# Decay rates of a gated recurrence in a PSUM bank, and the gates' plus-one on ScalarE

## The chip, the cores and the metric

The kernel runs on one core of one Trainium2 chip. The metric is the device time in microseconds (us) of one execution, as the median over runs.

Names used below: PE is TensorE, whose weight loads are listed apart as PEld; DVE is VectorE, ACT is ScalarE, POOL is GpSimd, and SP is SyncE, which issues most of the DMAs. SBUF is the working memory. PSUM is the memory that PE writes its products to, and here it is handled in eight banks of 128 partitions by 512 float32 numbers.

## The reference

One block of a decoder on a sequence of 512 positions with 1024 channels, all in float32. Cut to what matters here:

```python
h = rmsnorm(x, norm1_g[l])
z = h @ w_in[l] + b_in[l]
z_glu, z_rx, z_rg, z_ga, z_gb = jnp.split(z, split_idx, axis=-1)
u = z_glu[..., :D_CONV] * jax.nn.sigmoid(z_glu[..., D_CONV:])
u = causal_depthwise_conv(u, conv_dw_w[l], conv_dw_b[l])
u = jax.nn.silu(layernorm(u, conv_ln_g[l], conv_ln_b[l]))
y_a = u @ conv_w_out[l] + conv_b_out[l]
xb = causal_depthwise_conv(z_rx, lru_conv_w[l], lru_conv_b[l])
hb = rg_lru(xb, ...)
y_b = (hb * jax.nn.gelu(z_rg, approximate=True)) @ lru_w_out[l]
m = jax.nn.sigmoid(z_ga) * y_a + jax.nn.sigmoid(z_gb) * y_b
x = x + m @ w_mix_out[l]
```

The first conv has 31 taps, the second 4. A second norm, a SwiGLU feed-forward of 2816 channels and a last norm follow. The recurrence `rg_lru` works on 1280 channels. It forms two gates r and i from block-diagonal products of xb, and from the parameter `lru_lambda` the decay of each channel:

```python
log_a = -LRU_C * r * jax.nn.softplus(-lam)
a = jnp.exp(log_a)
mult = jnp.sqrt(-jnp.expm1(2.0 * log_a))
```

With these h[t] = a[t] * h[t-1] + mult[t] * i[t] * xb[t], and LRU_C is 8. So `softplus(-lam)`, one number for each channel, is needed once for the whole kernel (1280 numbers, held as 128 partitions by 10). The change concerns these ten columns, and one operation of the ten gate units.

## The kernel before

**Layout.** Channels lie on the 128 partitions and the 512 positions along the free dimension. Every matrix is cut into tiles of 128 output channels. To keep float32 accuracy, each operand is split into a high part and a low remainder, and each product is three matmuls (high by high, high by low, low by high; `mm3`, L539). The high part is a cast on ACT (`split_to`, L133), the remainder a subtraction on DVE or POOL (L129). For most weight chunks of w_in POOL does the subtraction.

**Order of the work.** After a hand-ordered start (L638 to L669: the input norm, its transposes, the first four tiles u0 and u1 of the input product), a written list `ORDER` says in which order the units come: `u` (two input tiles and the gated product, `glu`, L796), `rx` (an input tile and the four-tap conv, `rx`, L810), `g` (the gates of one of ten tiles, `gates`, L845), `r` (the recurrence of one tile, `recur`, L879), `rg`, `gb` and `ga` (further input tiles with their activations, L895 and L888). It begins `u0 u1 rx0 rx1 gb0 rx2 u2 g0 rx3 gb1 g1` and ends `rg9 ga2 ga3 ga4 ga5 ga6 ga7`. Then come the products with lru_w_out (`yb`), conv_w_out (`co`, `ya`), the mixing product (`mx`), and the feed-forward (`f`, `fr`, `o`).

**The side work.** The 31-tap conv, 240 instructions `scalar_tensor_tensor` on DVE (L733) for four pairs of tiles, and after it the layer norm are a generator, `beside()` (L721). Each unit of `ORDER` advances it by some steps (`run_beside(n)`, L789), and from rg5 on its steps are ordered behind the product of an earlier `rg` unit (`behind`, L787 and L899). Its two column sums are matmuls by ones (`column_mean`, L740, tiles `lnmp` and `lnvp`), each called a fixed count of steps (`LAG` = 12) after its input.

**Who orders the queues.** The text gives a priority; the framework fixes the order in each engine's queue when the kernel is built, from its own estimate of times. Each engine then works through its queue in order and waits at its head for semaphores. Outside the hand-ordered parts, work that stands later in the text can so come earlier in a queue.

**PSUM.** A pool `psum` of six banks (`bank`, tag mm) serves the input tiles, the gates and the recurrence, and a pool of two (`bank2`) serves the conv accumulators. A bank is held from its first writer to its last reader.

**What the change touches.** L674 to L699 compute the rates ahead of the first unit: x = -lambda, its absolute value, e = exp(-|x|) on ACT (L680), s = e / (2 + e), a polynomial in s squared of nine terms (L686 to L690) that makes log(1 + e), softplus = max(x, 0) + 2 * s * polynomial (L691), then `c8` and `c4`, the rates scaled by -4 and -2 (L694, L695). L699 halves the two gate biases into `bh`. All are instructions on 128x10 numbers in the SBUF tile `sm`, DVE except L680. The first readers are the gates of tile 0: L865 and L866 (Tanh, with `bh`), L869 (Exp, with `c8`) and L870 (Tanh, with `c4`).

In `gates` four DVE instructions follow: L871 makes r_ = (A + 1) * r_ in the PSUM bank, L872 the gated input, L873 writes A = r_ + 1 to SBUF, and L874 th = (A + 1) * r_, which `recur` turns into the factor `mult` (L882). L874 is the last reader of that bank. The copies of parts of xb that the gates of other tiles need (`ext_in`, L828) go by DMA through SP (L840); the gates read them in their fourth and later matmuls (L860).

Of the kernel before, what the change touches and what calls it, by code (L numbers as in the profile page):

```python
# [22 lines left out]
LRU_C = 8.0  # L23
# [4 lines left out]
NR = DR // P  # L28
# [68 lines left out]
def tile_block(ctx, tc, a, out):  # L97
    nc = tc.nc
    pool = lambda name, bufs, **k: ctx.enter_context(tc.tile_pool(name=name, bufs=bufs, **k))
    consts = pool("consts", 1)  # L100
# [16 lines left out]
    def bank(name):  # L117
        return psum.tile([P, T], F32, tag="mm", name=name)
# [4 lines left out]
    vec, act, pe, pool_e = nc.vector, nc.scalar, nc.tensor, nc.gpsimd  # L123
# [547 lines left out]

    lam = par[:, col["lru_lambda"] : col["lru_lambda"] + NR]  # L674
    sm = consts.tile([P, 6, NR], F32, name="sm")
    ab, e, s, s2, po, c4 = (sm[:, i, :] for i in range(6))
    vec.tensor_scalar(out=e, in0=lam, scalar1=-1.0, scalar2=None, op0=ALU.mult)
    vec.tensor_tensor(out=ab, in0=lam, in1=e, op=ALU.max)
    vec.tensor_scalar(out=c4, in0=e, scalar1=0.0, scalar2=None, op0=ALU.max)
    act.activation(e, ab, AF.Exp, scale=-1.0)  # L680
    vec.tensor_scalar(out=s, in0=e, scalar1=2.0, scalar2=None, op0=ALU.add)
    vec.reciprocal(s, s)
    vec.tensor_tensor(out=s, in0=s, in1=e, op=ALU.mult)
    vec.tensor_tensor(out=s2, in0=s, in1=s, op=ALU.mult)
    n_terms = 9
    vec.tensor_scalar(out=po, in0=s2, scalar1=1.0 / (2 * n_terms - 1), scalar2=1.0 / (2 * n_terms - 3), op0=ALU.mult, op1=ALU.add)  # L686
    for k in range(n_terms - 3, -1, -1):
        vec.tensor_tensor(out=po, in0=po, in1=s2, op=ALU.mult)
        vec.tensor_scalar(out=po, in0=po, scalar1=1.0 / (2 * k + 1), scalar2=None, op0=ALU.add)
    vec.tensor_tensor(out=po, in0=po, in1=s, op=ALU.mult)  # L690
    vec.scalar_tensor_tensor(out=c4, in0=po, scalar=2.0, in1=c4, op0=ALU.mult, op1=ALU.add)  # L691

    c8 = consts.tile([P, NR], F32, name="c8")
    vec.tensor_scalar(out=c8, in0=c4, scalar1=-LRU_C / 2, scalar2=None, op0=ALU.mult)  # L694
    vec.tensor_scalar(out=c4, in0=c4, scalar1=-LRU_C / 4, scalar2=None, op0=ALU.mult)  # L695

    bh = consts.tile([P, 2, NR], F32, name="bh")
    for g, name in enumerate(("lru_ba", "lru_bx")):
        vec.tensor_scalar(out=bh[:, g, :], in0=par[:, col[name] : col[name] + NR], scalar1=0.5, scalar2=None, op0=ALU.mult)  # L699

    def b_in(m):
        return pc("b_in", m)
# [86 lines left out]
    def run_beside(n):  # L789
        with tc.issue_after(behind[0]) if behind[0] else nullcontext():  # L790
            for _ in range(n):
                next(side, None)
        behind[0] = behind[1] or behind[0]


    def glu(j):  # L796
        pv = in_mm(GLU + j)
        run_beside(6 if j > 1 else 0)
        pg = in_mm(GLU + 8 + j)
        sg = shortt(f"sg{j}")  # L800
        act.activation(sg, pg, AF.Sigmoid, bias=b_in(GLU + 8 + j))
        uj = longt(f"u{j}")
        vec.scalar_tensor_tensor(out=uj, in0=pv, scalar=b_in(GLU + j), in1=sg, op0=ALU.add, op1=ALU.mult)
        u.append(uj)
        run_beside(6 if j else 0)
# [4 lines left out]
    def rx(j):  # L810
        ps = in_mm(RX + j)
        act.activation(ps, ps, AF.Identity, bias=b_in(RX + j))
        o = longt(f"xb{j}")
        lw = lambda s: pc("lru_conv_w", (KL - 1 - s) * NR + j)
        act.activation(o, ps, AF.Identity, scale=lw(0), bias=pc("lru_conv_b", j))
        for s in range(1, KL):
            vec.scalar_tensor_tensor(out=o[:, s:], in0=ps[:, : T - s], scalar=lw(s), in1=o[:, s:], op0=ALU.mult, op1=ALU.add)
# [27 lines left out]
    def gates(j):  # L845
        hv, lv = (gate_view(v[:, 0, :]) for v in weights(f"gate{j}"))
        j5 = j % 5
        banks = []
        for g in range(2):
            ps = bank(f"g{j}_{g}")  # L850
            (wh, oh), (wl, ol) = ((v[:, g, 0, :], v[:, g, 1, :]) for v in (hv, lv))
            xh, xl = xbp[j]
            mms = [(wh, xh), (wh, xl), (wl, xh)]
            if j5 % 2:
                eh, el = ext[j]
                mms += [(l[:MANY], r[:MANY]) for l, r in ((oh, eh), (oh, el), (ol, eh))]
            else:
                mms.append((oh[: 3 * FEW], ext[j][0][: 3 * FEW]))
            for k, (l, r) in enumerate(mms):
                pe.matmul(ps, l, r, start=k == 0, stop=k == len(mms) - 1)  # L860
# [8 lines left out]
        act.activation(A, th, AF.Exp, scale=c8[:, j : j + 1], bias=c8[:, j : j + 1])  # L869
        act.activation(r_, th, AF.Tanh, scale=c4[:, j : j + 1], bias=c4[:, j : j + 1])  # L870
        vec.scalar_tensor_tensor(out=r_, in0=A, scalar=1.0, in1=r_, op0=ALU.add, op1=ALU.mult)  # L871
        vec.scalar_tensor_tensor(out=xb[j], in0=i_, scalar=1.0, in1=xb[j], op0=ALU.add, op1=ALU.mult)  # L872
        vec.tensor_scalar(out=A, in0=r_, scalar1=1.0, scalar2=None, op0=ALU.add)  # L873
# [21 lines left out]
    def rg(j):  # L895
        ps = in_mm(RG + j)
        act.activation(ps, ps, AF.Gelu_apprx_tanh, bias=b_in(RG + j))
        product = vec.tensor_tensor(out=ps, in0=hs[j], in1=ps, op=ALU.mult)
        behind[1] = product.ins if j >= BEHIND else None  # L899
        y.append(split(f"y{j}", ps, vec))  # L900
# [4 lines left out]
    for kind, j in ORDER:  # L905
        next(f_sums_steps, None)
        if kind == "u":
            glu(j)
        elif kind == "rx":
            rx(j)  # L910
            run_beside(4)
        elif kind == "g":
            gates(j)
        elif kind == "r":
            recur(j)
        elif kind == "rg":
            rg(j)
            run_beside(6)
        elif kind == "gb":
            sig(GB, j, sgb, "sgb")  # L920
            run_beside(6)
        else:
            sig(GA, j, sga, "sga")
            run_beside(8)


    for j in range(8):
        ws = w_tiles(f"lo{j}_0", 5) + w_tiles(f"lo{j}_1", 5)
        ps = bank(f"yb{j}")
# [121 lines left out]
    for n, j in enumerate(mixq.order()):  # L1051
        ws = w_tiles(f"co{j}", ND)
        ps = bank(f"ya{j}")
# [410 lines left out]
```

## Time and profile before

| what | value |
|---|---|
| median of 3 runs | 799.04 us (797.56 to 799.54) |
| the profiled execution: span from first to last instruction | 797.3 us |
| that execution's own time beside its span | not given apart from the span; the median lies 1.7 us above it |
| mean granted clock of PE | 0.997 of full speed |
| busy share of the span: PE, DVE, ACT, POOL | 99%, 87%, 59%, 45% |
| instructions | 12582 |

How to read the rows that follow. A row of the timeline is: start in us, duration in us (of the whole group where it ends in x2 or more), engine, line of the kernel, operation, tile written <- tiles read, shapes, count; in square brackets the idle time of that engine just before it, and what ended it. A row of grouped instructions ends with busy us and mean ns of one, then idle time before. A row of waits is: engine, what waited, what it waited for, us in total, times, longest. A row of the table by stage is: the stretch in us, its length, then for PE, PEld, DVE, ACT and POOL the busy us with the count of instructions, and the granted clock, the DMA share and GB/s. PE's weight loads run beside its matmuls.

### The profile page before, as it was taken

Reading aid. Unit: us, or ns where it says so; the run is one execution under the profiler, and the core shown is the slowest. Engines: PE = TensorE matmul, PEld = TensorE weight load, DVE = VectorE, ACT = ScalarE, POOL = GpSimd, SP = SyncE. Lnnn points to the kernel's source line nnn. Section 1 sums busy time; section 2 is a strip of 40 time slices with the busy share of each in tenths; the row PEclk is TensorE's granted clock in tenths of the full one; section 3 lists DMA queues with packets and bytes.
Section 4 is the critical chain, followed back from the end, with each engine's and each line's share of the span. In section 5 each row is a group of like instructions: output and inputs, shape, how many; then the busy total and the mean of one; then the engine's idle time right before and its main releaser. Section 6 shows DMA issues by size and latency. Waiting matters only on the chain.

```text
span 797.3 us, 12582 instructions
## 1 busy us (share of the span) xinstructions
PE 786.5 (99%) x4374; PEld 689.1 (86%) x4374; DVE 696.8 (87%) x1097; ACT 473.2 (59%) x674; POOL 359.9 (45%) x347
## 2 busy tenths in 40 slices
PE   8999999999999999999999999999999999999996
PEld 7988888888888888888887898999999999888885
DVE  5899999999998997985799968898877798999956
ACT  7546688777679654562326467554555555556743
POOL 2576778788779988853360482113312221000000
PEclk9999999999999999999999999999999999999998
DMA  7745566577776786879887887588988898778652
GB/s 216 196 127 175 162 190 195 179 238 229 200 247 202 243 272 212 281 232 296 266 309 238 277 263 230 150 273 264 355 298 289 301 326 294 239 236 258 206 171 105
DMA packets 181074, 188.13 MB, mean 236 GB/s; under 512 B 14119, under 2 KB 142035, under 8 KB 181011
## 3 DMA queue, kind: packets, MB, share of 16 engines
q1 hardware_dynamic: 172195, 156.66, 63.1%
q0 software_dynamic: 8672, 30.41, 11.0%
q8 instruction: 34, 0.56, 0.3%
q10 hardware_dynamic: 144, 0.26, 0.1%
q14 instruction: 29, 0.24, 0.1%
HBM read 145.48 MB, written 38.80 MB: 231 GB/s over the span
## 4 chain that ended last, share of the span: by engine, by line
PE 83%; DVE 9%; DMA 4%; issue 2%; ACT 2%; SPq 0%; DVEq 0%; ACTq 0%
PE z L539 35%; PE fr L1218 24%; PE or L991 13%; PE f L539 3%; PE g L860 3%; PE mxr L991 3%; DMA raw_lo<-in_lru_w_out_dram 1%; DMA raw_co<-in_conv_w_out_dram 1%; DMA mxws<-in_w_mix_out_dram 1%; PE fr L1262 1%; DVE hl_co L129 1%; PE yb L539 1%; DVE hl_mxb L129 1%; DVE mxws L129 1%; DVE sga L1056 1%
## 5 line engine op out<-in xcount | busy, mean ns | idle before, releaser
L733 DVE SCALAR_TENSOR_TENSOR cv<-u,par,cv 128x511 f32<-128x511 f32 (+17 forms) x240 | 162.6, 728 | 1.1 <-ACT cv L730 0.9
L129 POOL TENSOR_TENSOR hl_in<-raw_in,hl_in 128x1024 fp32r<-128x1024 f32 x51 | 123.2, 2422 | 63.6 <-ACT hl_in L133 45.1
L129 POOL TENSOR_TENSOR fws<-fws 128x256 f32<-128x256 f32 x120 | 104.6, 874 | 78.6 <-DMA fws<-in_ffn_w_dram 72.9
L398 POOL DMA_DIRECT2D ot<-fwso x21 | 15.3, 731 | 164.4 <-DVE fwso L129 156.7
L1218 PE MATMUL fr<-hs_0h,hl_ft 128*128 128x256 f32 x320 | 59.2, 283 | 0.0
L133 ACT CAST hl_in<-raw_in 128x1024 fp32r<-128x1024 f32 x51 | 53.2, 1043 | 3.2 <-POOL fws L394 1.3
L129 DVE TENSOR_TENSOR hl_ft<-raw_ft,hl_ft 128x1024 fp32r<-128x1024 f32 x39 | 47.5, 1218 | 5.5 <-ACT hl_ft L133 5.5
L1218 PEld LDWEIGHTS fr<-hs_0h,hl_ft 128*128 128x128 f32 x320 | 50.6, 192 | 0.0
L133 ACT CAST hl_ft<-raw_ft 128x1024 fp32r<-128x1024 f32 x40 | 41.8, 1046 | 13.2 <-PE fr L1218 9.9
L129 DVE TENSOR_TENSOR hl_fb<-raw_fb,hl_fb 128x1024 fp32r<-128x1024 f32 x30 | 36.7, 1222 | 14.6 <-ACT hl_fb L133 13.8
L1218 PE MATMUL fr<-hs_0l,hl_ft 128*128 128x256 f32 x160 | 45.3, 283 | 0.0
L133 ACT CAST hl_fb<-raw_fb 128x1024 fp32r<-128x1024 f32 x30 | 31.5, 1050 | 20.8 <-PE fr L1218 13.3
L539 PE MATMUL z<-h10h,hl_in 128*128 128x512 f32 (+1 forms) x110 | 41.4, 378 | 0.0
L539 PE MATMUL z<-h17h,hl_in 128*128 128x512 f32 (+1 forms) x110 | 41.1, 376 | 0.0
L539 PE MATMUL z<-h11h,hl_in 128*128 128x512 f32 (+1 forms) x110 | 41.1, 376 | 0.0
L539 PE MATMUL z<-h13h,hl_in 128*128 128x512 f32 (+1 forms) x110 | 41.1, 376 | 0.0
L539 PE MATMUL z<-h14h,hl_in 128*128 128x512 f32 (+1 forms) x110 | 41.1, 376 | 0.0
L539 PE MATMUL z<-h15h,hl_in 128*128 128x512 f32 (+1 forms) x110 | 41.1, 376 | 0.0
L539 PE MATMUL z<-h16h,hl_in 128*128 128x512 f32 (+1 forms) x110 | 41.1, 376 | 0.0
L539 PE MATMUL z<-h12h,hl_in 128*128 128x512 f32 (+1 forms) x110 | 41.1, 375 | 0.0
L133 ACT CAST hl_ob<-raw_ob 128x1024 fp32r<-128x1024 f32 (+1 forms) x23 | 23.4, 1016 | 23.4 <-PE or L991 10.5
L394 POOL TENSOR_TENSOR fws<-fws 128x256 f32<-128x256 f32 x40 | 31.6, 792 | 2.8
(962 smaller groups left out, 2640.6 us busy)
## 6 DMA issues: line engine op xcount, KB each, us to landing
raw_in<-in_w_in_dram SPq DMA_DIRECT2D x52, 512.0 KB
fws<-in_ffn_w_dram SPq DMA_DIRECT2D x80, 256.0 KB
raw_ft<-fs SPq DMA_DIRECT2D x34, 512.0 KB
fs<-fws SPq DMA_DIRECT2D x23, 512.0 KB
ot<-fwso POOLq DMA_DIRECT2D x21, 512.0 KB, 6.0
fwso<-in_ffn_w_dram POOLq DMA_DIRECT2D x40, 256.0 KB, 7.1
fs<-fws POOLq DMA_DIRECT2D x17, 512.0 KB, 4.9
raw_ob<-in_ffn_w_dram SPq DMA_DIRECT2D x33, 256.0 KB
```

The costliest lines, as they stand in the source:

```text
L129: return eng.tensor_tensor(out=o, in0=x, in1=y, op=ALU.subtract)
L133: copy(h, full)
L394: eng.tensor_tensor(out=q11, in0=q22, in1=q11, op=ALU.add)
L398: return queue.dma_start(dest, raw.rearrange("p (m n) -> p m n", m=dest.shape[1]))
L539: pe.matmul(ps, l, r, start=i == 0, stop=i == n - 1)
L733: vec.scalar_tensor_tensor(out=acc[c][:, s:], in0=u[c][:, : T - s], scalar=dw(c, s), in1=acc[c][:, s:], op0=ALU.mult, op1=ALU.add)
L860: pe.matmul(ps, l, r, start=k == 0, stop=k == len(mms) - 1)
L991: pe.matmul(banks[i], l_[:, ts], r_, start=start and n == 0, stop=stop and n == 2, skip_group_check=again)
L1056: vec.scalar_tensor_tensor(out=o, in0=ps, scalar=pc("conv_b_out", j), in1=o, op0=ALU.add, op1=ALU.mult)
L1218: pe.matmul(ps[:, HALVES[i]], lw[:, c, :], rx_, start=not (again or i or c or m), stop=bool(i and c == 3 and m == 2), skip_group_check=True,)
L1262: pe.matmul(self.r4[:, HALVES[i]], lw, rx_, start=not (i or c or m), stop=bool(i and c == 3 and m == 2), skip_group_check=True)
```

## The change

The rates move into a function `decay_rates`, called in the loop over `ORDER` after unit rx0 and its four steps of side work. Four of its intermediate columns lie in a bank of the six (`bank("sm")`), the others in SBUF, so that each DVE instruction has an operand in PSUM. The polynomial is now one `scalar_tensor_tensor` for each term, (po + coefficient) * s2, in place of a multiplication and an addition. ACT takes over 2 + e, the square, the first coefficient and the two halvings. In `gates` the plus-one of L873 becomes a Copy with a bias on ACT.

```diff
-    lam = par[:, col["lru_lambda"] : col["lru_lambda"] + NR]
-    sm = consts.tile([P, 6, NR], F32, name="sm")
-    ab, e, s, s2, po, c4 = (sm[:, i, :] for i in range(6))
...
-    act.activation(e, ab, AF.Exp, scale=-1.0)
-    vec.tensor_scalar(out=s, in0=e, scalar1=2.0, scalar2=None, op0=ALU.add)
-    vec.reciprocal(s, s)
...
-    vec.tensor_scalar(out=po, in0=s2, scalar1=1.0 / (2 * n_terms - 1), scalar2=1.0 / (2 * n_terms - 3), op0=ALU.mult, op1=ALU.add)
-    for k in range(n_terms - 3, -1, -1):
-        vec.tensor_tensor(out=po, in0=po, in1=s2, op=ALU.mult)
-        vec.tensor_scalar(out=po, in0=po, scalar1=1.0 / (2 * k + 1), scalar2=None, op0=ALU.add)
-    vec.tensor_tensor(out=po, in0=po, in1=s, op=ALU.mult)
-    vec.scalar_tensor_tensor(out=c4, in0=po, scalar=2.0, in1=c4, op0=ALU.mult, op1=ALU.add)
...
+    sm = consts.tile([P, 4, NR], F32, name="sm")
+    c4, c8 = (consts.tile([P, NR], F32, name=n) for n in ("c4", "c8"))
     bh = consts.tile([P, 2, NR], F32, name="bh")
-    for g, name in enumerate(("lru_ba", "lru_bx")):
-        vec.tensor_scalar(out=bh[:, g, :], in0=par[:, col[name] : col[name] + NR], scalar1=0.5, scalar2=None, op0=ALU.mult)
+
+    def decay_rates():
+
+        lam = par[:, col["lru_lambda"] : col["lru_lambda"] + NR]
+        ps = bank("sm")
+        neg, ab, inv, po = (ps[:, i * NR : i * NR + NR] for i in range(4))
+        lo, e, s, s2 = (sm[:, i, :] for i in range(4))
+        vec.tensor_scalar(out=neg, in0=lam, scalar1=-1.0, scalar2=None, op0=ALU.mult)
+        vec.tensor_tensor(out=ab, in0=lam, in1=neg, op=ALU.max)
+        vec.tensor_scalar(out=lo, in0=neg, scalar1=0.0, scalar2=None, op0=ALU.max)
+        act.activation(e, ab, AF.Exp, scale=-1.0)
+        act.activation(inv, e, AF.Copy, bias=2.0)
+        vec.reciprocal(inv, inv)
+        vec.tensor_tensor(out=s, in0=inv, in1=e, op=ALU.mult)
+        act.activation(s2, s, AF.Square)
+        n_terms = 9
+        act.activation(po, s2, AF.Copy, scale=1.0 / (2 * n_terms - 1))
+        for k in range(n_terms - 2, 0, -1):
+            vec.scalar_tensor_tensor(out=po, in0=po, scalar=1.0 / (2 * k + 1), in1=s2, op0=ALU.add, op1=ALU.mult)
+        vec.scalar_tensor_tensor(out=po, in0=po, scalar=1.0, in1=s, op0=ALU.add, op1=ALU.mult)
+        vec.scalar_tensor_tensor(out=po, in0=po, scalar=2.0, in1=lo, op0=ALU.mult, op1=ALU.add)
+        vec.tensor_scalar(out=c8, in0=po, scalar1=-LRU_C / 2, scalar2=None, op0=ALU.mult)
+        vec.tensor_scalar(out=c4, in0=po, scalar1=-LRU_C / 4, scalar2=None, op0=ALU.mult)
+        for g, name in enumerate(("lru_ba", "lru_bx")):
+            act.activation(bh[:, g, :], par[:, col[name] : col[name] + NR], AF.Copy, scale=0.5)
...
-        vec.tensor_scalar(out=A, in0=r_, scalar1=1.0, scalar2=None, op0=ALU.add)
+        act.activation(A, r_, AF.Copy, bias=1.0)
         vec.scalar_tensor_tensor(out=th, in0=A, scalar=1.0, in1=r_, op0=ALU.add, op1=ALU.mult)
...
             rx(j)
             run_beside(4)
+            if j == 0:
+                decay_rates()
```

More of the change, by code (lines that the diff above doesn't have):

```diff
@@ L670, in tile_block @@
     h1 = parts_of(h1p)
-    lam = par[:, col["lru_lambda"] : col["lru_lambda"] + NR]
-    sm = consts.tile([P, 6, NR], F32, name="sm")
-    ab, e, s, s2, po, c4 = (sm[:, i, :] for i in range(6))
-    vec.tensor_scalar(out=e, in0=lam, scalar1=-1.0, scalar2=None, op0=ALU.mult)
-    vec.tensor_tensor(out=ab, in0=lam, in1=e, op=ALU.max)
-    vec.tensor_scalar(out=c4, in0=e, scalar1=0.0, scalar2=None, op0=ALU.max)
-    act.activation(e, ab, AF.Exp, scale=-1.0)
-    vec.tensor_scalar(out=s, in0=e, scalar1=2.0, scalar2=None, op0=ALU.add)
@@ L682, in tile_block @@
-    vec.reciprocal(s, s)
-    vec.tensor_tensor(out=s, in0=s, in1=e, op=ALU.mult)
-    vec.tensor_tensor(out=s2, in0=s, in1=s, op=ALU.mult)
-    n_terms = 9
-    vec.tensor_scalar(out=po, in0=s2, scalar1=1.0 / (2 * n_terms - 1), scalar2=1.0 / (2 * n_terms - 3), op0=ALU.mult, op1=ALU.add)
-    for k in range(n_terms - 3, -1, -1):
-        vec.tensor_tensor(out=po, in0=po, in1=s2, op=ALU.mult)
-        vec.tensor_scalar(out=po, in0=po, scalar1=1.0 / (2 * k + 1), scalar2=None, op0=ALU.add)
-    vec.tensor_tensor(out=po, in0=po, in1=s, op=ALU.mult)
@@ L691, in tile_block @@
-    vec.scalar_tensor_tensor(out=c4, in0=po, scalar=2.0, in1=c4, op0=ALU.mult, op1=ALU.add)
-    c8 = consts.tile([P, NR], F32, name="c8")
-    vec.tensor_scalar(out=c8, in0=c4, scalar1=-LRU_C / 2, scalar2=None, op0=ALU.mult)
-    vec.tensor_scalar(out=c4, in0=c4, scalar1=-LRU_C / 4, scalar2=None, op0=ALU.mult)
-    bh = consts.tile([P, 2, NR], F32, name="bh")
-    for g, name in enumerate(("lru_ba", "lru_bx")):
-        vec.tensor_scalar(out=bh[:, g, :], in0=par[:, col[name] : col[name] + NR], scalar1=0.5, scalar2=None, op0=ALU.mult)
+    sm = consts.tile([P, 4, NR], F32, name="sm")
```

## The prediction

> **What bounds the kernel now.** I read the page first, then the busy time by stage, then what TensorE (PE) waited for.
>
> ```profile
> span 797.3 us, 12582 instructions
> PE 786.5 (99%) x4374; PEld 689.1 (86%) x4374; DVE 696.8 (87%) x1097; ACT 473.2 (59%) x674; POOL 359.9 (45%) x347
> ```
>
> ```profile
> core 0: us, PE busy (x) PEld busy (x) DVE busy (x) ACT busy (x) POOL busy (x), PEclk, DMA share, GB/s
> 0.00:25.00 25.00, 22.31 (x160) 20.77 (x161) 13.56 (x38) 18.32 (x43) 7.85 (x9) 1.00 0.74 215
> ```
>
> ```profile
> 686.00:787.00 101.00, 101.00 (x447) 83.66 (x446) 90.22 (x145) 60.39 (x91) 0.72 (x1) 1.00 0.65 208
> 787.00:797.30 10.30, 3.65 (x17) 2.68 (x15) 5.12 (x11) 3.26 (x9) 0.00 (x0) 0.80 0.27 102
> ```
>
> ```profile
> 25.00:37.70 12.70, 12.70 (x102) 12.43 (x101) 11.64 (x30) 5.11 (x6) 7.70 (x4) 1.00 0.82 220
> 37.70:68.90 31.20, 31.20 (x139) 25.84 (x138) 29.64 (x47) 14.34 (x20) 20.11 (x14) 1.00 0.46 132
> 68.90:231.00 162.10, 162.10 (x715) 134.01 (x714) 158.30 (x240) 119.27 (x149) 126.29 (x107) 1.00 0.69 206
> ...
> 355.00:395.00 40.00, 40.00 (x178) 33.15 (x177) 25.36 (x33) 10.73 (x15) 12.01 (x14) 1.00 0.89 288
> 395.00:438.50 43.50, 42.12 (x186) 34.29 (x184) 42.95 (x67) 21.70 (x31) 16.46 (x18) 1.00 0.81 275
> ```
>
> ```profile
> PE mxr L991 <- DVE x L940: 1.4, 1, 1.4
> ```
>
> PE is busy in 786.5 of 797.3 us, which leaves 10.8 us without it. The stage table says where: 25.00 - 22.31 = 2.7 us in the first 25, 43.50 - 42.12 = 1.4 us before 438.5, and 10.30 - 3.65 = 6.65 us at the very end; together 10.75. Busy could hide waiting, so I check the pace: 715 matmuls in 162.10 us is 0.227 us each, and 447 in 101.00 us is 0.226, far from the change, at a granted clock of 1.00 in both. A stretch that held stalls would be slower than the other. So from 25 us to 437 us PE runs without a break, and VectorE (DVE), though busy in 158.3 of 162.1 us, is behind it, not ahead.
>
> The change edits work between 25 and 252 us. The first 2.7 us and the last 6.65 us lie outside its reach. What it could win is the one wait at 437, 1.4 us, and nothing else that this profile shows: the best case is 0.2%.
>
> **The change part by part.**
>
> *The decay rates.* The rows to look at are the small DVE instructions beside those of GpSimd (POOL).
>
> ```profile
> 25.36 0.17 DVE L677 TENSOR_SCALAR sm<-par 128x10 f32<-128x10 f32 x1
> 25.44 0.24 DVE L699 TENSOR_SCALAR bh<-par 128x10 f32<-128x10 f32 x2
> ...
> 27.18 2.34 DVE L688 TENSOR_TENSOR sm<-sm 128x10 f32<-128x10 f32 x1
> 29.56 2.34 DVE L689 TENSOR_SCALAR sm<-sm 128x10 f32<-128x10 f32 x1
> ...
> 37.64 0.74 DVE L803 SCALAR_TENSOR_TENSOR u<-z,par,sg 128x512 f32<-128x512 f32 x1
> ```
>
> ```profile
> 27.10 4.77 POOL L129 TENSOR_TENSOR hl_in<-raw_in,hl_in 128x1024 fp32r<-128x1024 f32 x2 [4.62 <-ACT hl_in L133]
> ```
>
> ```profile
> L688 DVE TENSOR_TENSOR sm<-sm 128x10 f32<-128x10 f32 x7 | 5.5, 789 | 0.2
> L689 DVE TENSOR_SCALAR sm<-sm 128x10 f32<-128x10 f32 x7 | 3.8, 537 | 0.2
> ```
>
> ```profile
> 30.55 0.69 ACT L801 ACTIVATE sg<-z,par 128x512 f32<-128x512 f32 x1 [0.48 <-PE z L539]
> ```
>
> Today 28 DVE instructions run from 25.36 to 37.64, that is 12.3 us, ahead of the first gated product, u0 (L803). Undisturbed, one is busy 0.17 us and the next starts 0.04 us later (27.18 + 2.34 to 29.56), a step of 0.21. Two took 2.34 us and ended, at 31.90, with the two POOL instructions beside them (27.10 + 4.77 = 31.87). By the grouped rows the fourteen of L688 and L689 took 5.5 + 3.8 = 9.3 us, where 14 x 0.17 makes 2.4: waits of 6.9 us, over half of the block.
>
> The new block has 16 DVE instructions: 3 ahead of Exp, the reciprocal, the product s, 7 steps of the polynomial, 2 that finish it, 2 scalings, which is 16. Six go to ScalarE (ACT). Each DVE one has an operand in PSUM. No 128x10 instruction of the trace touches PSUM, so I bound its step from both sides: 0.17 us at least, if not even the 0.04 between two remain, and 0.7 us at most, that of the 128x512 rows below, which read and write PSUM. I take 0.21, from the rows of its own size: 16 x 0.21 = 3.4 us, 11.2 at the upper bound. DVE saves 12.3 - 3.4 = 8.9 us, 1.1 at worst.
>
> [...]
>
> When does the block run? Its operands are ready at 25.36, and the queue's order is not the program's: L699 ran before the third instruction of the chain that stands above it. So it may fill the gap until u0's sigmoid ends at 31.24, as before; or it stands between taps at some 45 to 60 us, as its place in the program says. Either way PE has its work. In the second case ACT must load the table for Exp and then the old one again:
>
> ```profile
> 71.76 1.28 ACT L869 ACT_TABLE_LOAD   x1
> 73.06 0.82 ACT L869 ACTIVATE ea<-th,c 128x512 f32<-128x512 f32 x1
> ```
>
> Two loads of 1.28 and six small instructions at about 0.21 (DVE's step, for want of a nearer row) are 3.8 us. The cover is ACT's idle time from 37.7 to 68.9, 31.20 - 14.34 = 16.9 us; without it the casts of weights behind them would be up to 3.8 us late. The first reader of the rates is g0's Tanh, whose successor loads its table at 71.76, so the block has until 70 us.
>
> [...]
>
> The block also borrows one of six PSUM banks, for 3.4 us and the hops to ACT if it runs in one piece, for some 16 x (0.21 + 0.65) = 14 us if a tap of 0.65 stands before each of its instructions. Who else holds one then?
>
> ```profile
> 50.90 0.74 DVE L817 SCALAR_TENSOR_TENSOR xb<-z,par,xb 128x509 f32<-128x509 f32 x1
> ...
> 58.31 0.74 DVE L817 SCALAR_TENSOR_TENSOR xb<-z,par,xb 128x509 f32<-128x509 f32 x1
> ```
>
> These are the last readers of rx0's and rx1's banks. A unit of 24 matmuls lasts 24 x 0.227 = 5.4 us, so between the two rows gb0 and rx2, perhaps u2, hold one too: at most four of six. The fifth costs nothing; if all six were taken, PE would wait for the block's end.
>
> *The plus-one*, ten times:
>
> ```profile
> L873 DVE TENSOR_SCALAR ea<-g x10: 674/680/691, 78.8 to 251.1; 128x512 f32<-128x512 f32 x10
> 309.40 0.59 ACT L745 ACTIVATE lnmp<-lnmp 128x512 f32<-128x512 f32 x1
> ```
>
> DVE loses 10 x 0.68 = 6.8 us. ACT gains ten Copies; L745 is a Copy from PSUM at 0.59 us; the Exp of L869 above, which writes SBUF and reads two pointers, takes 0.82. I take 0.65, near the Copy: 6.5 us, with 5.9 and 8.2 as the ends. From 68.9 to 231 ACT is idle for 162.10 - 119.27 = 42.8 us, which hides it. The new wait is one hop: DVE's L874 now waits for ACT, which stands behind whatever ACT has queued. Behind L874 on DVE wait conv taps and the steps of the next rx unit.
>
> *The sum.* DVE is relieved of 8.9 + 6.8 = 15.7 us (8 to 16). Where does that go?
>
> ```profile
> 242.07 0.69 DVE L898 TENSOR_TENSOR z<-xb,z 128x512 f32<-128x512 f32 x1 [2.15 <-ACT z L897]
> 310.03 2.48 DVE L129 TENSOR_TENSOR u<-u,lnmp 128x512 f32<-128x512 f32 x4 [3.59 <-ACT lnmp L745]
> 390.76 0.69 DVE L129 TENSOR_TENSOR mxws<-mxws,mxws 128x512 f32<-128x512 f32 x1 [1.90 <-DMA mxws<-in_w_mix_out_dram]
> ```
>
> At 242 DVE already waits 2.15 us for rg5, which PE makes, and the taps of the last pair are put behind that product. All but g9's plus-one is saved before it, so 15.0 us only lengthen that wait and earlier ones. What follows, 0.7 us, meets the wait at 310: the mean of the layer norm is two matmuls that stand in PE's order behind ga5, and PE is never early. From 355 to 395 DVE is idle for 40.00 - 25.36 = 14.6 us, at 390.76 for a DMA. So DVE reaches 395 when it did, and the 1.4 us at 437 stay. Gain: 0. The profiled span of 797.3 lies 1.7 us under the median of 799.04 (the three runs go from 797.56 to 799.54); I forecast the median, **799.0 us**.
>
> **The rivals.**
>
> *The wait at 437 closes.* The sums of the layer norm or the order of the queues could move forward with a lighter DVE, and the additions at L940 would be in time: 799.0 - 1.4 = 797.6 us. For it: DVE is busy for 42.95 of the 43.50 us before. Against it: the waits at 310 and 390, which nothing in the change shortens.
>
> *The hop stalls PE.* The narrowest place is after g4:
>
> ```profile
> 142.14 0.68 DVE L871 SCALAR_TENSOR_TENSOR g<-ea,g 128x512 f32<-128x512 f32 x1
> 145.38 0.66 ACT L897 ACTIVATE z<-z,par 128x512 f32<-128x512 f32 x1 [1.84 <-PE z L539]
> 145.97 1.04 ACT L133 CAST hl_in<-raw_in 128x1024 fp32r<-128x1024 f32 x1
> 151.55 1.53 SPq L840 DMA_DIRECT2D ext<-xb6h  x2
> 156.22 1.85 PE g L860 x8
> ```
>
> ```profile
> fs<-fws POOLq DMA_DIRECT2D x17, 512.0 KB, 4.9
> ```
>
> Were g4's plus-one put behind that gelu and cast, it would end at 147.0 + 0.65 = 147.7 rather than 144.2 (1.36 us after L871 ended, by one tap and L873), 3.5 us late. L874, the steps of rx6 behind it, xb6 and its copies would follow, and g5 needs the third of these, issued by 152.3, with its fourth matmul at 156.2 + 3 x 0.23 = 156.9. Of these 4.6 us the copy's landing takes a part: less than 4.6, as PE doesn't wait today, though 512 KB take 4.9. A landing of 4 us leaves a lead of 0.6, and PE would stall for 3.5 - 0.6 = 2.9 us; with no landing at all it wouldn't stall. It decides from a hop that is late by the lead. I take 2.9, as the one DMA row is long: 801.9 us. Against it: the queues need not be ordered so, and ACT has idle time at 143.5, just when L871 is done.
>
> *It doesn't do what it says*: the block fills the gap at 25 and no taps are delayed. That gives 799.0 too and is part of the forecast.
>
> **How the numbers follow.** Forecast, PE unmoved: 0.67. Wait at 437 gone: 0.12. The hop: 0.15. The remaining 0.06 are orders of the queues that no row lets me price, as likely on either side. A measurement of this kernel can tell about 0.3%, 2.4 us, from no change. Faster by more than that: half of the rest and little of the second case, 0.05. Slower: the hop and the other half, 0.17. Within: 0.78. The range takes in the wait gone, 797.6 less 0.4 for the spread of the runs, and the hop: **797.2 to 801.9**.
>
> **What would show it.** Right: no DVE instruction of 128x10 over 0.7 us; u0 at about 31 instead of 37.64; the wait before rg5's product at 242 longer, and PE still at 715 matmuls in 162.1 us from 68.9. The wait at L940 still 1.4. Wrong: any wait of PE between 25 and 320, first at g5's matmuls near 157; or lnmp's matmul elsewhere than behind ga5, which moves all that follows.

## The result, and the profile after

| kernel | median, us | executions, us | ratio to before, 95% interval |
|---|---|---|---|
| before | 798.25 | 797.56 to 801.92 (7) | 1 |
| after | 803.48 | 801.18 to 805.51 (7) | 1.0056 [1.0035, 1.0078] |

The change makes the kernel slower by 0.56% (4.5 us by that ratio; the two medians are 5.2 us apart), and its median lies outside the predicted range of 797.2 to 801.9. The profiled execution of after took 804.07 us, with a span of 802.3, 5.0 us over that of before.

First the parts of the forecast that held. The page of after:

```profile
PE 788.3 (98%) x4374; PEld 689.9 (86%) x4374; DVE 683.5 (85%) x1075; ACT 481.1 (60%) x691; POOL 356.6 (44%) x347
```

The timeline of after (line numbers are 2 higher from the taps on):

```profile
31.62 0.75 DVE L805 SCALAR_TENSOR_TENSOR u<-z,par,sg 128x512 f32<-128x512 f32 x1 [5.95 <-ACT sg L803]
35.48 0.16 DVE L684 TENSOR_SCALAR sm<-par 128x10 f32<-128x10 f32 x1
...
49.50 0.18 DVE L695 SCALAR_TENSOR_TENSOR sm<-sm 128x10 f32<-128x10 f32 x1
...
58.58 0.15 DVE L699 TENSOR_SCALAR c<-sm 128x10 f32<-128x10 f32 x1
```

DVE was relieved of 696.8 - 683.5 = 13.3 us. No small instruction is stretched any more (0.15 to 0.22 us each), u0 runs at 31.62 instead of 37.64, and the block stands between taps from 35.5 to 58.6. The relief itself came. Now the stages, first of before, in stretches that were not shown, then of after:

```profile
40.00:460.00 420.00, 418.62 (x1851) 345.88 (x1850) 388.57 (x567) 260.75 (x345) 284.92 (x256) 1.00 0.73 227
180.00:200.00 20.00, 20.00 (x90) 16.54 (x89) 19.24 (x30) 15.64 (x21) 17.34 (x17) 1.00 0.76 229
200.00:460.00 260.00, 258.62 (x1147) 213.54 (x1146) 231.58 (x330) 147.26 (x201) 162.41 (x157) 1.00 0.80 252
438.50:510.00 71.50, 71.41 (x431) 63.67 (x432) 60.65 (x107) 42.76 (x75) 30.23 (x34) 1.00 0.77 232
```

```profile
40.00:460.00 420.00, 415.05 (x1824) 341.82 (x1823) 377.24 (x556) 263.68 (x350) 274.40 (x251) 1.00 0.73 225
68.90:231.00 162.10, 160.36 (x706) 132.29 (x705) 148.82 (x225) 122.58 (x156) 122.89 (x103) 1.00 0.65 193
180.00:200.00 20.00, 19.27 (x85) 15.59 (x83) 15.69 (x25) 12.28 (x16) 15.93 (x15) 1.00 0.56 167
200.00:460.00 260.00, 255.77 (x1122) 210.43 (x1123) 230.15 (x325) 151.02 (x202) 161.33 (x157) 1.00 0.80 253
438.50:510.00 71.50, 68.20 (x396) 59.27 (x395) 60.68 (x106) 43.63 (x77) 30.22 (x34) 1.00 0.80 247
```

In the prediction's terms: 706 matmuls from 68.9 instead of 715, so PE did stall there. Two places lose: 160.36 of 162.10 us busy, and 68.20 of 71.50. (Before lost 1.4 us too, just ahead of 438.5, so some 1.9 us of the second are new.) The DVE column says where the relief went. From 40 to 460 DVE is busy for 11.3 us less than before (377.24 against 388.57), from 200 to 460 for only 1.4 us less (three plus-ones are left there). So from 40 to 200 DVE is busy for 9.9 us less; a part of that is work which came late and was still undone at 200. The stage from 180 to 200 is the worst: DVE, ACT and POOL all do less, and the DMA engines move 167 GB/s instead of 229, which over 20 us is 1.2 MB.

The waits of PE in after:

```profile
PE mxr L995 <- DVE x L944: 3.2, 2, 1.8
PE z L539 <- DVE y3l L129: 1.7, 1, 1.7
```

The same matmuls in before, then in after. PE's order is the same in both, so starts can be compared one by one.

```profile
198.54 0.39 PE L539 MATMUL z<-h17h,hl_in 128*128 128x512 f32 x1
198.77 0.39 PE L539 MATMUL z<-h10h,hl_in 128*128 128x512 f32 x1
...
438.50 0.73 PE L991 MATMUL mxr<-hl_mxt,mxvb0h 128*128 128x512 f32 x2 [1.38 <-DVE x L940]
```

```profile
198.88 0.39 PE L539 MATMUL z<-h17h,hl_in 128*128 128x512 f32 x1
201.01 0.50 PE L539 MATMUL z<-h10h,hl_in 128*128 128x512 f32 x1 [1.74 <-DVE y3l L129]
...
440.90 0.71 PE L995 MATMUL mxr<-hl_mxt,mxvb0h 128*128 128x512 f32 x2 [1.83 <-DVE x L944]
443.21 0.73 PE L995 MATMUL mxr<-hl_mxt,mxvb0h 128*128 128x512 f32 x2 [1.38 <-DVE x L944]
```

PE is 0.34 us behind at 198.88 (all of it from the start of the execution), 2.2 us behind at the first matmul of rx9, and 4.7 behind at 443.21. The stall at rx9 is the wait for a PSUM bank: in both kernels the build gave rx9 the bank of rg3, whose last reader is the subtraction y3l (in e6 below, the kernel before with one edit, rx9 waits for y3l too). Before, y3l was done three microseconds early; now it is late. The next fences follow it back to its cause, before first. Each has ACT, then POOL, then DVE:

```profile
175.23 1.04 ACT L133 CAST hl_in<-raw_in 128x1024 fp32r<-128x1024 f32 x1
179.94 0.59 ACT L133 CAST y2h<-z 128x512 fp32r<-128x512 f32 x1 [3.68 <-DVE z L898]
176.34 2.40 POOL L129 TENSOR_TENSOR hl_in<-raw_in,hl_in 128x1024 fp32r<-128x1024 f32 x1 [2.81 <-ACT hl_in L133]
185.83 0.81 DVE L218 CAST hl_gate<-raw_gate 32x256 fp32r<-32x256 f32 x1 [0.72 <-POOL hl_gate L129]
195.15 0.68 DVE L129 TENSOR_TENSOR y3l<-z,y3h 128x512 fp32r<-128x512 f32 x1
```

```profile
179.01 0.59 ACT L133 CAST y2h<-z 128x512 fp32r<-128x512 f32 x1 [1.41 <-DVE z L900]
179.49 1.05 ACT L133 CAST hl_in<-raw_in 128x1024 fp32r<-128x1024 f32 x1
180.62 2.40 POOL L129 TENSOR_TENSOR hl_in<-raw_in,hl_in 128x1024 fp32r<-128x1024 f32 x1 [6.73 <-DMA raw_gate<-in_lru_wx_dram]
189.68 0.80 DVE L218 CAST hl_gate<-raw_gate 32x256 fp32r<-32x256 f32 x1 [4.28 <-POOL hl_gate L129]
200.28 0.68 DVE L129 TENSOR_TENSOR y3l<-z,y3h 128x512 fp32r<-128x512 f32 x1
```

Look at the order of the two casts of ACT. Before, the weight chunk in14 is cast at 175.23 and y2h, which needs DVE's product, waits behind it at no cost to anyone. In after, y2h stands ahead, ACT waits 1.41 us for the product, and in14 is cast at 179.49, 4.3 us later. (POOL's row names a DMA; but that cast ended at 180.54, 0.08 us before POOL began.) POOL waits 6.7 us instead of 2.8, DVE waits at the head of its own queue for POOL (L218, 4.28 us; all waits of L218 grow from 3.9 to 9.7 us), and y3l ends 5.1 us later: 3.9 of these stand at L218 already, the rest is two more taps that DVE's queue now has ahead of y3's product. Nothing in this chain is an instruction of the change.

### The profile page after: what moved, and what is told of

It reads as the page before. It is cut to its first block, busy times and chain, and to the rows that moved or that the text cites. A ratio compares the mean times of both kernels' runs of the same rounds, so it can differ in the third digit from the quotient of the medians.

```text
span 802.3 us, 12563 instructions
## 1 busy us (share of the span) xinstructions
PE 788.3 (98%) x4374; PEld 689.9 (86%) x4374; DVE 683.5 (85%) x1075; ACT 481.1 (60%) x691; POOL 356.6 (44%) x347
## 4 chain that ended last, share of the span: by engine, by line
PE 74%; DVE 13%; DMA 6%; issue 3%; ACT 2%; POOL 2%; SPq 1%; POOLq 0%; DVEq 0%; ACTq 0%
PE z L539 27%; PE fr L1222 24%; PE or L995 13%; DVE cv L735 3%; PE f L539 3%; PE mxr L995 3%; PE g L862 2%; DMA mxws<-in_w_mix_out_dram 2%; DMA raw_co<-in_conv_w_out_dram 1%; DVE mxws L129 1%; PE fr L1266 1%; PE yb L539 1%; POOL hl_in L129 1%; DVE hl_mxb L129 1%; DMA raw_lo<-in_lru_w_out_dram 1%
## 5 line engine op out<-in xcount | busy, mean ns | idle before, releaser
L735 DVE SCALAR_TENSOR_TENSOR cv<-u,par,cv 128x507 f32<-128x507 f32 (+15 forms) x240 | 162.4, 732 | 3.1 <-ACT cv L732 3.1
L129 POOL TENSOR_TENSOR fws<-fws 128x256 f32<-128x256 f32 x120 | 101.4, 848 | 81.2 <-DMA fws<-in_ffn_w_dram 75.7
L394 POOL TENSOR_TENSOR fws<-fws 128x256 f32<-128x256 f32 x40 | 32.2, 806 | 2.8
```

Of the source, the lines that this page charges most:

```text
L129: return eng.tensor_tensor(out=o, in0=x, in1=y, op=ALU.subtract)
L394: eng.tensor_tensor(out=q11, in0=q22, in1=q11, op=ALU.add)
L735: vec.scalar_tensor_tensor(out=acc[c][:, s:], in0=u[c][:, : T - s], scalar=dw(c, s), in1=acc[c][:, s:], op0=ALU.mult, op1=ALU.add)
```

## The experiments

The runs, all but the last but one timed against the kernel before on the same chip. All compute the whole reference. "Order" means the order in which the build writes each engine's queue.

| run | what | median, us | ratio to before, 95% interval |
|---|---|---|---|
| after_again | the changed kernel | 801.62 | 1.0051 [1.003, 1.0071] |
| e1_moved | decay block alone | 806.26 | 1.0095 [1.0076, 1.0113] |
| e2_plus1 | plus-one alone | 802.61 | 1.006 [1.0039, 1.0081] |
| e3_y2_later | changed, y2h behind in14 | 801.91 | 1.0037 [1.0017, 1.0056] |
| e5_newform | decay block rewritten at its old place | 798.61 | 0.9995 [0.998, 1.001] |
| e6_y2_first | before, y2h ahead of in14 | 802.22 | 1.004 [1.0025, 1.0055] |
| e7_adds_first | changed, additions first | 803.95 | 1.0066 [1.0049, 1.0082] |
| e8_adds_first_b | before, additions first | 799.08 | 1.0002 [0.9983, 1.0021] |
| e10_plus1_copies | plus-one alone, copies behind casts | 800.47 | 1.0025 [1.0009, 1.004] |
| e12_both_ordered | whole change, y2h and copies behind casts | 797.92 | 0.9997 [0.9978, 1.0015] |
| e1_again | e1_moved, one execution | 803.92 | none |
| e13_before_ordered | before, the two edits of e12 | 804.42 | 1.0065 [1.0043, 1.0087] |

**The changed kernel again.** 

> The changed kernel once more, to see whether its waits are its own. Its first profile shows TensorE waiting some 2.0 us at 199 to 201 for the bank of the fourth rg unit (rg3, read last by the subtraction y3l) and 3.6 us (1.4 before) at the additions ahead of mxr. Theory (a fixed queue order: ScalarE's cast of the weight chunk in14 stands behind the cast y2h, which waits for VectorE): the same two waits at the same places, median 803 to 804, ratio about 1.0056. Rival (chance: a late DMA in one execution): the wait at 199 to 201 is absent in some executions, so the second profile shows another place or none and the times spread from 798 up.

The median, 801.62, is lower than the theory's 803 to 804; the ratio, 1.0051, is close to its 1.0056. The wait at rx9 came back at the same place (1.8 us for y3l), and again in e7, whose queues are those of after up to the additions. So it belongs to the queues and not to one late transfer. The waits for the additions were 1.6 us together, but PE lost about as much in another way, in the stages around 438:

```profile
437.93:441.34 3.41, 1.80 (x7) 0.92 (x6) 3.41 (x7) 2.40 (x4) 0.00 (x0) 1.00 1.05 377
441.34:444.75 3.41, 3.41 (x9) 2.68 (x8) 3.41 (x6) 1.96 (x4) 0.00 (x0) 0.50 1.17 317
```

Behind 3.41 us in which PE was busy for only 1.80, the granted clock fell to 0.50 for just 3.41 us: 9 matmuls where 3.41 / 0.227 = 15 would fit, and a loss of half the stretch, some 1.7 us. The 1.6 us of waits then cost some 3.3.

**One half alone.**

```diff
-        act.activation(A, r_, AF.Copy, bias=1.0)
+        vec.tensor_scalar(out=A, in0=r_, scalar1=1.0, scalar2=None, op0=ALU.add)
```

> The decay block moved and rewritten alone; the plus-one is VectorE's again. In this build the cast of in14 stands ahead of y2h in ScalarE's queue, as in the kernel before. Theory: no wait of TensorE near 200, GpSimd's wait ahead of in14's subtraction about 3 us as before instead of 6.7, additions' wait ahead of mxr 1 to 2 us, 798.3 (797.5 to 799.5). Rival (the block between the taps or its PSUM bank is what costs): the wait near 200 remains and the time is 801 to 804.

The other half is the kernel before with the reverse of this edit:

> The plus-one on ScalarE alone; the decay rates as before. The cast of in14 stands ahead of y2h here too. Theory: no wait near 200, 798.3 (797.5 to 799.5). Rival (the hop through ScalarE in each of ten gates is what costs): TensorE waits at a g unit or near 200, 801 to 804.

Both expectations missed: each half alone is slower, and the decay block alone by more than the whole change. Read narrowly (in14 and y2h alone), my theory fell here. The traces show the same kind of fault at other places. ACT in e1_moved, with POOL's subtraction:

```profile
174.72 0.59 ACT L738 COPY u<-cv 128x512 f32<-128x512 f32 x1 [2.90 <-DVE cv L735]
...
180.02 0.59 ACT L738 COPY u<-cv 128x512 f32<-128x512 f32 x1
180.50 1.05 ACT L133 CAST hl_in<-raw_in 128x1024 fp32r<-128x1024 f32 x1
181.63 2.41 POOL L129 TENSOR_TENSOR hl_in<-raw_in,hl_in 128x1024 fp32r<-128x1024 f32 x1 [8.13 <-DMA raw_gate<-in_lru_wx_dram]
```

ACT in e2_plus1, with the matmul that waited for it:

```profile
229.37 0.58 ACT L736 COPY u<-cv 128x512 f32<-128x512 f32 x1 [6.07 <-DVE cv L733]
...
231.27 0.69 ACT L801 ACTIVATE sg<-z,par 128x512 f32<-128x512 f32 x1
232.01 0.50 PE L539 MATMUL z<-h10h,hl_in 128*128 128x512 f32 x1 [1.22 <-ACT sg L801]
```

Here it is the copy of a finished conv accumulator that waits for DVE's last tap at the head of ACT's queue, with the cast of in14 behind it in the one and the sigmoid of u7 in the other. In before, the copies of the first case stood in front of an earlier chunk (168.37, the cast at 169.05), and those of the second stood behind u7 (237.62). For e2 this is only a part of the account: its profiled execution, 800.39, is the fourth fastest of twelve and lost 1.5 us there, while six others took 803.3 to 807.1 and have no trace. e1_moved once more:

> The decay block moved and rewritten alone, once more for a second profile: its first one, 802.87, was the fastest of six executions (median 806.3). Theory A: the same chain (a copy of the conv ahead of the cast of in14, GpSimd's wait of 8 us there, the bank of rg3 late for rx9) with a longer wait of TensorE at 200 and a halved clock behind it, 804 to 807. Rival: a wait at a place that the first profile does not show, which would be a cost of the block itself.

It shows the same copy and the same 8.1 us of POOL; PE waited 0.4 us for y3l and, new, 1.6 us between 360 and 385 for weight chunks (hl_lo, hl_co) and 2.7 for the additions, at a clock of 1.00 throughout. The time, 803.92, is just under the forecast. The wait is not where I expected it, at 200, but later, and the first profile of e1_moved doesn't have those of 360 to 385, which is what the rival named. But e13 below, which has this order and no decay block between the taps, waits for hl_co there as well (0.8 us), so these waits are not a cost of the block itself.

**The order repaired in one place.** Three lines move y2's split behind the input matmuls of rx8:

```diff
+        if j == 8:
+            later.pop()()
...
-        y.append(split(f"y{j}", ps, vec))
+        later.append(lambda: y.append(split(f"y{j}", ps, vec)))
+        if j != 2:
+            later.pop()()
```

> The changed kernel with one thing moved: the split of rg2's product (y2h, y2l) is issued after the input matmuls of rx8, so that ScalarE casts in14 first and y2h second, the order of the kernel before. Both parts of the change stay, and the banks and TensorE's order stay. Theory: GpSimd's wait ahead of in14's subtraction falls from 6.7 to about 3 us, y3l ends near 196 instead of 200.3, the 2 us of TensorE at 199 to 201 are gone and the additions' wait ahead of mxr falls from 3.6 to 1.4 to 2.5: 798.3 to 800. Rivals (the hop, or the block between taps and its bank): as the changed kernel, 803 to 804.

POOL's wait fell to 4.7 us, y3l began at 199.50 with the whole execution 1.4 us late from its start, and PE lost 0.2 us at rx9 instead of 2.0. The time was 801.91, not 798.3 to 800: in the trace the loss at rx9 went, and the additions (2.6 us, with the clock at 0.50 behind them) kept the rest. The intervals of e3 and after overlap, so the runs alone don't show that it gained.

**The same instructions in the old order.** The rewritten block is called ahead of the first unit, the plus-one stays on DVE:

```diff
             if j == 0:
-                decay_rates()
...
+    decay_rates()
```

> The rates in their new form (PSUM bank, one instruction for each term, ScalarE's share), but called where they stood before, ahead of the first unit; the plus-one stays on VectorE. The queues of all engines keep the order of the kernel before behind the block. Theory A (what costs is the new order in which the queues are written, not the instructions): no wait of TensorE from 25 to 437, 798.3 (797.5 to 799.3). Theory B (the new instructions or the borrowed bank cost by themselves): 800 to 803, with a wait between 25 and 200.

As the kernel before: 0.9995. Up to 456 us PE, ACT, DVE and POOL work in the order of before, the block apart. The new instructions, the borrowed bank (here held for 6 us, ahead of the taps) and ACT's share cost nothing, and relieve DVE as meant. POOL in e5, then DVE (two answers of the same timeline):

```profile
28.17 7.15 POOL L129 TENSOR_TENSOR hl_in<-raw_in,hl_in 128x1024 fp32r<-128x1024 f32 x3 [5.78 <-ACT sm L688]
29.50 1.44 DVE L695 SCALAR_TENSOR_TENSOR sm<-sm 128x10 f32<-128x10 f32 x7 [0.85 <-ACT sm L693]
31.55 0.74 DVE L807 SCALAR_TENSOR_TENSOR u<-z,par,sg 128x512 f32<-128x512 f32 x1
```

Seven steps in 1.44 us, 0.21 each, beside POOL's instructions that had held the old ones for 2.34. None of these seven, each with an operand in PSUM, was held. In before L688, with two inputs from SBUF, and L689, with one, both took 2.34 us beside them. What in the new form spares the steps was not separated: the operand in PSUM and the instruction itself came together.

**The inversion alone, without the change.**

```diff
+            with tc.issue_after(newest["y2"]) if key == "in14" else nullcontext():
                 h, l = split_to(hl[:, 0, :n], hl[:, 1, :n], rv, lo, act.copy if emitted[0] > 1 else vec.tensor_copy)
```

> The kernel before, with one inversion put into it: on ScalarE the cast of the weight chunk in14 stands behind y2h, as the changed kernel has it; nothing of the change is in it. Theory A (order): GpSimd's wait ahead of in14's subtraction rises from 2.8 us, y3l ends later than 195, the DMA engines move about 1 MB less by 200, TensorE waits 0 to 2 us at rx9 and 1.4 to 3 us at the additions ahead of mxr: 799.5 to 803. Theory B (the change's own instructions): nothing of it moves, 798.3.

POOL, DVE and PE of e6, then its stages:

```profile
181.69 2.42 POOL L129 TENSOR_TENSOR hl_in<-raw_in,hl_in 128x1024 fp32r<-128x1024 f32 x1 [8.03 <-ACT hl_in L133]
200.73 0.68 DVE L129 TENSOR_TENSOR y3l<-z,y3h 128x512 fp32r<-128x512 f32 x1
201.46 0.50 PE L540 MATMUL z<-h10h,hl_in 128*128 128x512 f32 x1 [2.41 <-DVE y3l L129]
```

```profile
180.00:200.00 20.00, 19.05 (x84) 15.40 (x82) 15.09 (x24) 12.34 (x17) 15.72 (x14) 1.00 0.50 148
202.53:205.94 3.41, 3.41 (x10) 2.64 (x9) 3.41 (x6) 2.27 (x3) 3.25 (x6) 0.51 0.88 267
```

One cast moved behind y2h makes the whole picture: POOL's wait, y3l, the stall at rx9, 148 GB/s. Up to 456 us ACT's order differs from that of before in this one place; the build also moved a subtraction and a memset of POOL and a few taps of DVE between 182 and 203, the subtraction just as in after. In this execution the clock halved behind the stall as well, so PE was 4.5 us behind at 210. At 438 it got 1.7 of them back, because the wait of before for the additions fell away. Over all six executions that makes 802.22, by 0.40% slower than before with no instruction of the change in it.

**The second wait.** Can it be removed at its place? The four additions go ahead of four splits in DVE's queue:

```diff
-                if k >= self.lag:
+                if last_mx:
+                    with tc.issue_after(added):
+                        for _ in range(3):
+                            split_late()
+                elif k >= self.lag and not (n == "mx" and k):
                     split_late()
```

> The changed kernel with the four additions that free mxr's banks put ahead of four splits in VectorE's queue (those of mxeb1, mxvb1 and the weight chunk b22_2). It takes away the second wait and leaves the first. Theory A (two separate waits, and a halved clock for 3.4 us behind the second in some executions): the 2.0 us at rx9 stay, the wait ahead of mxr falls from 3.2 to under 1 us, the clock stays at 1.00 there, 800 to 801.3. Theory B (all of the loss comes from the wait at rx9, what follows is its echo): 803, as the changed kernel, the loss moving to a later wait.

> The kernel before with the same four additions put ahead. It has one wait, 1.4 us. Theory A: the wait goes, 796.9 (796.2 to 797.8), and no execution is far above the others. Theory B: the splits behind the additions are late in their turn and TensorE waits for them, 798 to 799.

In both the wait moved, as theory B had it, and the times are its own (803.95; 799.08 against 798 to 799). e8's trace, of the slowest of its twelve executions, has four waits for the additions, 2.5 us together. That all of the loss comes from rx9, as B says for e7, is not shown: in e7's profiled execution the clock halved behind rx9 as well. PE in e7:

```profile
457.03 0.50 PE L995 MATMUL mxr<-mxt40h,mxvb0h 128*128 128x512 f32 x1 [1.60 <-DVE x L944]
```

From 395 to 438.5 DVE is busy for 42.95 of 43.5 us, so what is put first makes the next late. What counts there is when DVE arrives at that stretch. In before it did so behind a DMA at 390.76; after:

```profile
395.57 0.69 DVE L129 TENSOR_TENSOR mxws<-mxws,mxws 128x512 f32<-128x512 f32 x1 [0.29 <-DMA mxws<-in_w_mix_out_dram]
```

That is 4.8 us later, and 1.2 MB that were not moved from 180 to 200 are 4.5 us at the 275 GB/s of that stretch. The sizes agree, but the other traces do not bear it out: after_again, with 166 GB/s from 180 to 200, has this subtraction at 392.55; e5, with 228 and the order of before, at 391.78; e8, with 229, at 393.87. So the late transfer is not explained by that stretch alone.

What the traces do show is that its lateness against PE goes with the wait. Take how much later than in before the subtraction starts, less how much later PE is at the same matmul near 395 (e7 and e8, which move the additions, are left out):

| run | later than in before against PE, us | PE's waits for the additions, us |
|---|---|---|
| e12 | -2.6 | none |
| e6 | -1.6 | none |
| e2, e10 | -0.5 | 1.1 |
| after_again | -0.5 | 1.6 |
| before | 0 | 1.4 |
| e5 | 1.0 | 2.2 |
| e13 | 1.0 | 2.6 |
| e3 | 1.4 | 2.6 |
| e1_moved, e1_again | 1.5 | 2.7 |
| after | 2.4 | 3.2 |

As e5, whose median is that of before, waits 2.2 us in its profiled execution (800.18), not all of this wait is the change's.

**All of the change, with the orders repaired.** To e3's edit comes one for the copies of the conv; e10 has it with the plus-one alone:

```diff
-                act.copy(u[c], acc[c])
+                with tc.issue_after(newest["cast"]):
+                    act.copy(u[c], acc[c])
```

> The plus-one on ScalarE alone, and the copies that end a pair of the conv (u from cv, which wait for VectorE's last taps) held behind the newest cast of a weight chunk in ScalarE's queue. In the profile of the plus-one alone such a copy stood at 229 ahead of the sigmoid of u7, idled for 6.1 us and TensorE waited 1.2 us for that sigmoid. Theory A (an instruction of ScalarE that waits for VectorE stands ahead of one that TensorE or GpSimd needs): the wait at 229 to 236 is gone, 798.3 to 799.3 against 802.6. Theory B (the hop of the plus-one itself): 802 to 803 still, with a wait of TensorE behind a gate unit.

> The whole change, with y2h behind the cast of in14 and the conv's copies behind the newest weight cast. Theory A: no wait of TensorE of over 0.3 us between 25 and 430, GpSimd's wait ahead of in14's subtraction 3 to 4 us instead of 6.7, 798.3 to 800. It is not expected to be faster than the kernel before: VectorE's relief has no place to go, and what TensorE waits for at 437 to 460 hangs on the weight DMAs. Theory B: 802 to 804, as the changed kernel.

e10 lost the wait at 229 to 236 and came to 800.47, between its two theories: the ratio fell from 1.0060 to 1.0025, and the intervals just touch. The edit moved every copy of the conv, so the fall is not that one copy's alone. Its profiled execution (798.73) shows no wait of PE beyond that of before (1.1 us at the additions), and why others reach 803.8 stays open. e12 has every instruction of the change, the hop included, and takes what the kernel before takes. POOL's wait ahead of in14 is 4.8 us in it, not 3 to 4. Which of its two edits did how much was not separated. All of PE's waits in its profiled execution lie in the first 25 us, so there even the wait at 437 is gone; the median is 0.28 us below that of before, within the interval. Its stages are otherwise those of before:

```profile
68.90:231.00 162.10, 162.10 (x715) 133.99 (x714) 152.95 (x230) 123.04 (x156) 125.23 (x107) 1.00 0.67 202
180.00:200.00 20.00, 20.00 (x90) 16.54 (x89) 18.78 (x30) 13.89 (x19) 19.24 (x18) 1.00 0.74 226
200.00:460.00 260.00, 260.00 (x1157) 215.03 (x1156) 232.52 (x333) 151.36 (x207) 164.03 (x160) 1.00 0.81 253
```

**The two edits without the change.**

> The kernel before, without the change, with the two orders of the last experiment put into it: y2h behind the cast of in14, the conv's copies behind the newest weight cast. It answers whether the change itself gains anything once the orders are equal. Theory A (VectorE's relief is absorbed): 797.5 to 798.5, the same as the ordered change (797.92) and as the kernel before (798.2). Rival (the change gains, and the new order hides it): 799.5 or more here, so that the ordered change would be the faster of the two by over 0.2%.

804.42, far from the expected 798. The edits gave another order here than in e12. ACT in e13:

```profile
175.15 0.59 ACT L738 COPY u<-cv 128x512 f32<-128x512 f32 x1 [2.91 <-DVE cv L734]
...
180.46 0.59 ACT L738 COPY u<-cv 128x512 f32<-128x512 f32 x1
180.94 1.06 ACT L133 CAST hl_in<-raw_in 128x1024 fp32r<-128x1024 f32 x1
```

It is the order of e1_moved up to that cast, and POOL waits 8.14 us again. So the question it was made for (does the change gain anything once the orders are equal?) isn't answered by it; e5, with the order of before, answers it for the decay block: no gain that its interval could tell. But it shows once more that an order without any of the change's instructions costs as much as the change did, and that e12's two edits are no rule that helps everywhere.

## Why the prediction was wrong

**What held.** PE bounds the kernel (busy for 99% of the span before, 98% after). The block's sizes (16 steps of 0.2 us, no stretched instruction, u0 at 31.6), the place between taps, the 0.60 us of ACT's Copy (0.65 taken), the cover for the table loads, and DVE's relief (13.3 us on the page, 15.7 forecast). The new instructions and the borrowed bank cost nothing, though the bank was held for 23 us and not 14: e5 and e12. One small sum is off: the chance of a slower kernel, 0.15 and half of 0.06, is 0.18 and not 0.17.

The steps with a PSUM operand took 0.15 to 0.18 us in after (the reciprocal 0.22), much as those from SBUF in before where POOL held none (0.16 to 0.17, the reciprocal 0.22). In after, Exp starts 1.36 us after its table load (38.98 to 40.34), and the sigmoid of gb0 1.30 us after its own (54.59 to 55.89); in before the Exp of L869 starts 1.30 us after its load (71.76 to 73.06).

**The step that failed** is the sum: "Gain: 0", reached by "All but g9's plus-one is saved before it, so 15.0 us only lengthen that wait and earlier ones". That DVE's relief becomes waiting was right (it is busy for 9.9 us less from 40 to 200, and still no step of the chain above comes earlier). But the waits did not stay DVE's own. The step took the rest of the queues as they stood in the trace of before, and the change rewrote them: the build put instructions of ACT that wait for DVE ahead of ones that don't, and PE lost 1.9 us at rx9 in after. One such inversion alone, put into the kernel before (e6), costs 0.40%; all of the change with the orders repaired (e12) costs nothing. The price of such an inversion was not in the sum; it sat in "orders of the queues that no row lets me price, as likely on either side", at 0.06. Here it was neither rare nor even: the three orders that the build chose by itself (after, e1_moved, e2) were all slower, and of the five in which an edit set a place (e3, e6, e10, e12, e13) four were slower, one of them, e6, made to be so, and one level; by 0.25 to 0.95% in all. The prediction's own sign of being wrong, a wait of PE between 25 and 320, came true, at 199 and not near 157.

**The bank.** "At most four of six" counted how many banks were in use around the borrowed one. What stalled PE was one particular bank, given to rx9 when the kernel was built, with three microseconds to spare (y3l done at 195.8, needed at 198.8). No count could show that; the last reader of the bank's last user could.

**The wait at 437.** "So DVE reaches 395 when it did, and the 1.4 us at 437 stay" failed with the DMA behind it: 390.76 became 395.57 in after, 389.12 in e12. The forecast that the wait before rg5's product at 242 would grow failed too: it is 2.12 us in after, 2.15 before. DVE comes to it at 243.55 in after and at 239.92 in before, so nothing of the relief was left there.

**The rivals.** "The hop stalls PE" had the right sign and 2.9 us of the 4.5, but not the mechanism. In after no gate unit makes PE wait, L876 waited for the plus-one 0.7 us in all, and e12 has the hop without a loss. That the wait at 437 would close was wrong for after, where it grew from 1.4 to 3.2 us; in e12's trace it did close, with the transfer 2.6 us earlier against PE than in before.

**What stays open.** Why the build chose these orders: that it takes DVE to be earlier than it is on the chip, as it knows nothing of DVE's waits for POOL, is argued and not shown. What makes the transfer ahead of 395 late stays open too, and so do the slow executions of e2 and e10. And the split of the 4.5 us between the bank, the additions and the halved clock differs from one execution to the next.

## What to carry to other kernels

When a kernel's queues are ordered at build by estimated times, a change to one instruction's cost or place changes the order of many others; compare the queues before forecasting "nothing", and give that case a price. In an engine that works in order, look for instructions that wait for a busy neighbour and ask what stands behind them: a weight cast 4.3 us late here passed through three engines to a PSUM bank. Where an engine off the path is relieved and its waits only grow, expect nothing to be won (in e12 DVE was busy for 13.8 us less than in before, and the ratio was 0.9997), and let the range lean to the slow side.

## What the runs showed of the hardware

The granted clock falls to 0.50 for 3.41 us behind a stall, in some executions: behind the additions in after_again, e3 and e13, behind rx9 in e6 and e7, and in neither place in the profile of after, though its stalls are as long. Two stretches of the same length in after, counted off in steps of 3.41 us back from the fall of its clock at 799.11, at the end:

```profile
437.30:440.71 3.41, 1.76 (x7) 0.81 (x5) 3.41 (x6) 3.41 (x7) 0.00 (x0) 1.00 0.93 324
440.71:444.12 3.41, 1.84 (x7) 1.27 (x8) 3.41 (x7) 1.79 (x3) 0.00 (x0) 1.00 1.08 384
```

That a fall begins only at such a step is the author's assumption. Behind a stretch of 3.41 us in which PE was busy for 1.80 the clock fell (after_again), and behind one of 1.64 (e7, at rx9). Behind 1.76 and 1.84 in after it did not, nor behind 1.67 at rx9 in after and in after_again. So a fall can follow a stretch that is idle by half, and PE's busy time by the profile doesn't tell when. For this kernel, by an estimate from these rows, a stall of 2 us costs 2 us, or 3.7 with the 1.7 that one fall loses.
